# A hybrid encoder layer on one core: V kept in the scratch by pairs of heads, the third pattern's results by heads, and the gate from tanh

## The chip, the cores and the metric

The kernel runs on one core of one Trainium2 chip. The metric is the device time of one execution in microseconds (us). The times of before are the median of three runs; the profile is that of one more execution, taken by the hardware profiler, and has its own time.

## The reference: what is computed

One encoder layer over a sequence of 2048 tokens of width 1024, float32 in and out. The first third matters here: eight heads of width 64 attend in three dilated patterns, whose results are merged by their log-denominators, and beside them a gated depthwise convolution runs over 512 channels.

```python
DILATED_PATTERNS = ((128, 1), (512, 4), (2048, 16))

def dilated_sliding_attention(q, k, v):
    for window, d in DILATED_PATTERNS:
        half = window // (2 * d)
        o, lse = banded_attention(to_strided(q, d), to_strided(k, d), to_strided(v, d), half)
        outs.append(from_strided(o, d, B))
        lses.append(from_strided(lse, d, B))
    w = jax.nn.softmax(jnp.stack(lses, axis=0), axis=0)
    return jnp.sum(w[..., None] * jnp.stack(outs, axis=0), axis=0)

def conformer_conv(a, g, conv_w, conv_b, ln_g, ln_b):
    u = a * jax.nn.sigmoid(g)
    u = depthwise_conv(u, conv_w, width=31) + conv_b
    return jax.nn.silu(layernorm(u, ln_g, ln_b))
```

The rest is `h = x + [att || conv] W_out`, cross attention to 256 memory rows, a squared-ReLU MLP of width 4096 and a last RMSNorm.

## The kernel before

Nearly every product is made of three TensorE matmuls of 128x512 in a split of float32 into a high and a low part (`mm3`, L197 to L200): high by high, high by low, low by high. The work runs in stages, and within a stage generators are interleaved step by step (`weave`, L92); most of their steps are pinned behind the last TensorE instruction (`pinned`, L83), so that TensorE's order is the order of the code, while the other engines' queues are ordered when the program is built (`schedule_with_timeline_sim`, L1430).

- **Preparation** (about 0 to 218 us of the profile): the memory rows' products (`memory`), then x is transposed and split (`xprep`, L320), and the first gate halves (`glu`, L491) and the first q and k projections begin. `xprep` writes x back to the scratch in tiles `xts` from two buffers (L333 to L335). At its end `edges` (L710) zeroes the 256 rows before and after V in the scratch tensor `vtok` with two stores from one tile `zrow` of 16 partitions; `zrow` takes one of the two `raw` weight buffers, which the projections' weight loads use next.
- **Projections** (218 to 540): q, k and V (`lin_qk`, `lin_v` L544). V goes to the scratch as float16, for each head 65 columns of the high part (with a one for the denominator) and 65 of the low part: `VW` = 130 columns a head, 1040 a token, two bytes each. `lin_v` makes four heads (`g`) by 128 tokens (`t`) at a time and stores a block with rows of 1040 bytes (L576).
- **The first query block with the third pattern** (540 to 800): `att(0, far)` works through eight heads in pairs `pr`. For each head it does the third pattern over all 2048 tokens (`att_far`, L836) and the first and second pattern for the first 512 queries (`att_units`, L947). A unit is a chain over engines: scores on TensorE (L855, L856 or L992), mask and minimum on VectorE (L772), exp on ScalarE (L773), four transposes on TensorE (L779), high part on ScalarE (L782) and low part on VectorE (L783), products with V on TensorE (L787 to L789), and a copy out (L867, L869, L1010, L1012). The second halves of the gate (`glu` with tokens 1024 to 2047) and the first output weights are woven between (`rest`, L1100), and the first convolution block's layer norm with its Silu (L266).
- **Four blocks of 512 tokens** (`post`, L1204; 800 to the end): output projection, cross attention, MLP and last norm on TensorE, with the next block's attention (`att(p + 1)`) and convolution woven between.

What the change touches:

- `load_v` (L956) brings V for one pair of heads: the third pattern's as one transfer (L960), the first pattern's as five of 128 rows (L963 to L965), the second pattern's as eight (L968 to L971), one for each half `c` and residue `b`. Each run that is contiguous in the scratch is one token's two heads, 520 bytes.
- The third pattern's results go to `oscr[pr][1]` (L871), a tensor of 2048 tokens by both heads' 66 columns, one head and eight residues at a time, on ScalarE's own queue of transfers (ACTq); a contiguous run is 264 bytes. `combine` (L883) loads the second pattern's and third pattern's results as two transfers (L888 to L890).
- `glu` makes the gate with a Sigmoid on ScalarE (L508) and multiplies it on VectorE (L511); the convolution's weights `cw` (L160) come in `conv_unit` (L211).

Everything else goes through SyncE's queue (SPq, L57), in one order: weights, keys, queries, V, results. An instruction that issues a transfer holds its engine's queue until it may go.

Of the kernel before, what the change touches and what calls it, by code (L numbers as in the profile page):

```python
# [21 lines left out]
P = 128  # L22
S = 2048
D = 1024
H = 8
# [12 lines left out]
ROW = 66  # L38
VW = 130
VR = 8 * VW  # L40
# [7 lines left out]
def hybrid_layer(ctx, tc, A, out):  # L48
    nc = tc.nc
    ACT, DVE, POOL, PE = nc.scalar, nc.vector, nc.gpsimd, nc.tensor  # L50
# [5 lines left out]
    def dma(o, i, q=None):  # L56
        (q or nc.sync).dma_start(o, i)  # L57

    dr = pool("dram", DRAM)
# [16 lines left out]
    last = {}  # L76
# [30 lines left out]
    kscr = dr.tile([2, HD, H, 16, 160], F32R, name="kscr")  # L107
    qscr = dr.tile([2, HD, H, S], F32R, name="qscr")
    qfar = dr.tile([2, HD, H, 16, P], F32R, name="qfar")
    vtok = dr.tile([256 + S + 256, VR], F16, name="vtok")  # L110
    uscr = [dr.tile([P, 2080], F32, name=f"uscr{c}") for c in range(4)]
    xscr = [dr.tile([P, S], F32, name=f"xscr{k}") for k in range(KC)]
    cscr = [dr.tile([P, S], F32, name=f"cscr{c}") for c in range(4)]
    oscr = [[dr.tile([S, 2 * ROW], F32, name=f"oscr{p}_{q}") for q in (1, 2)] for p in range(4)]
    cath = [dr.tile([P, S], F32R, name=f"cath{k}") for k in range(KC)]
    catl = [dr.tile([P, S], F32R, name=f"catl{k}") for k in range(KC)]
    ascr = dr.tile([XH // 2, P, KC, 2 * NMEM], F32, name="ascr")
# [16 lines left out]
    cw = cst.tile([P, 4, 32], F32, name="cw")  # L134
# [10 lines left out]
    def setup():  # L145
        vecs, cwn = t2("vecs", F32, (64, P)), t2("cwn", F32, (32, DCONV))
        DVE.memset(vecs, 0.0)
        DVE.memset(cwn, 0.0)
        for nm, key in (("norm_mix_g", "mix"), ("norm_x_g", "x"), ("norm_mlp_g", "mlp"),
                        ("conv_b", "conv_b"), ("conv_ln_g", "ln_g"), ("conv_ln_b", "ln_b")):  # L150
            v = A[nm][0].rearrange("(k p) -> k p", p=P)
            dma(vecs[GV[key]:GV[key] + v.shape[0], :], v)
        dma(vecs[GV["final"]:GV["final"] + 8, :], A["norm_final_g"].rearrange("(k p) -> k p", p=P))
        dma(cwn[0:CW, :], A["conv_w"][0])
        pv = ps("c", "pvec")
        PE.transpose(pv[:, 0:64], vecs, ident[0:64, 0:64])
        for c in range(4):
            PE.transpose(pv[:, 64 + 32 * c:96 + 32 * c], cwn[:, c * P:(c + 1) * P], ident[0:32, 0:32])
        ACT.copy(gv, pv[:, 0:64])
        ACT.copy(cw.rearrange("p a b -> p (a b)"), pv[:, 64:192])  # L160

    def gain(key, k):
        if key == "mem":
# [114 lines left out]
    wp = pool("weights")  # L278
# [211 lines left out]

    def glu(c, ns, fine=False):  # L491

        sig = {}

        def unit(x, c0):
            raw = wp.tile([P, 8, P], F32, tag="raw", name=f"raw_{x}{c}{ns[0]}", bufs=2)
            dma(raw, wcols(w_in, c0))
            yield
            wh, wl = wsplit2(wp, raw, f"{x}{c}{ns[0]}", lo_eng=POOL)
            yield  # L500
            for n in ns:
                pt = ps("mm", "lin")
                for _ in linear_steps(pt, wh, wl, n):
                    if fine:
                        yield
                if x == "g":
                    sig[n] = t2(f"sig{c}_{n}")
                    ACT.activation(sig[n], pt, AF.Sigmoid)  # L508
                else:
                    u = t2(f"u{c}_{n}")  # L510
                    last["dve"] = DVE.tensor_tensor(u, pt, sig[n], op=ALU.mult)  # L511
                    dma(uscr[c][:, 15 + 512 * n:15 + 512 * (n + 1)], u)
                yield

        return unit("g", 3 * DATT + DCONV + c * P), unit("a", 3 * DATT + c * P)
# [28 lines left out]
    def lin_v(g, ns):  # L544

        raws = []
        for e in range(2):
            raws.append(wp.tile([P, 8, P], F32, tag="raw", name=f"raw_v{g}{e}", bufs=2))
            dma(raws[e], wcols(w_in, 2 * DATT + 256 * g + P * e))
        yield  # L550
        wh = lbv.tile([P, 8, 256], F32R, tag="wvh", name=f"wvh{g}{ns[0]}")
        wl = lbv.tile([P, 8, 256], F32R, tag="wvl", name=f"wvl{g}{ns[0]}")
        for e, raw in enumerate(raws):
            with ExitStack() as st:
                after(st, "pe")
                pc = ps("c", f"vbc{g}{e}")
                bcast_rows(pc, vmul[:, 2 * g + e:2 * g + e + 1], 1)
            DVE.tensor_tensor(raw, raw, pc[:, 0:P].unsqueeze(1).to_broadcast([P, KC, P]), op=ALU.mult)
            es = slice(e * P, (e + 1) * P)
            ACT.copy(wh[:, :, es], raw)  # L560
            POOL.tensor_tensor(wl[:, :, es], raw, f(wh[:, :, es]), op=ALU.subtract)
        yield
        for t in range(4 * ns[0], 4 * ns[-1] + 4):
            n, j = divmod(t, 4)
            pt = ps("mm", f"v{g}_{t}")[:, 0:256]
            for k in range(KC):
                sl = slice(j * P, (j + 1) * P)
                mm3(pt, XH_[k, n][:, sl], XL_[k, n][:, sl], wh[:, k, :], wl[:, k, :], k == 0, k == KC - 1)
            st = lbv.tile([P, 4, VW], F16, tag="vst", name=f"vst{g}_{t}", bufs=6)
            POOL.memset(st[:, :, HD:HD + 2], 1.0)  # L570
            p3 = pt.rearrange("p (h d) -> p h d", d=HD)
            ACT.copy(st[:, :, 0:HD], p3)
            last["dve"] = DVE.tensor_tensor(st[:, :, HD + 2:VW], p3, st[:, :, 0:HD], op=ALU.subtract)
            s2 = st.rearrange("p h e -> p (h e)")
            gs = slice(g * 4 * VW, (g + 1) * 4 * VW)
            dma(vtok[256 + P * t:256 + P * (t + 1), gs], s2)  # L576
            if t % 2:
                yield

# [128 lines left out]
        drain(*gens)  # L708

    def edges():  # L710
        zrow = wp.tile([16, 1, VR], F16, tag="raw", name="zrow", bufs=2)
        DVE.memset(zrow, 0.0)
        zb = zrow.to_broadcast([16, 16, VR])
        for t0 in (0, 256 + S):
            dma(vtok[t0:t0 + 256].rearrange("(q x) e -> q x e", q=16), zb)
        for c in range(4):
            dma(uscr[c][:, 0:15], zero[:, 0:15])
            dma(uscr[c][:, 15 + S:2080], zero[:, 0:17])
# [43 lines left out]
    aq = pool("att_q", side="right")  # L762
# [73 lines left out]
    def att_far(p2_, h, k, vt, q):  # L836

        pr, hh = divmod(h, 2)
# [3 lines left out]
        def unit(rq, qh, ql):  # L842
            if rq % 2 == 0:
                o8[0] = p2_.tile([P, 8, ROW], F32, tag="o3", name=f"o3_{h}{rq}", bufs=2)
            o2 = o8[0]
# [22 lines left out]
            else:  # L868
                DVE.tensor_copy(os_[:, :, 0:HD + 1], opt)  # L869
            if rq % 2:  # L870
                dma(oscr[pr][1].rearrange("(p r) (h e) -> p r h e", r=16, h=2)[:, 4 * rq - 4:4 * rq + 4, hh], o2,  # L871
                    nc.scalar)

        for rq in range(4):
            if rq == 0:
# [7 lines left out]
    def combine(p, pr, o0):  # L883
# [1 line left out]
        if p:  # L885
            yield
        ld = aq.tile([P, 2, 4, 2, ROW], F32, tag="ld", name=f"ld{p}{pr}")
        for i in range(2):  # L888
            dma(ld[:, i].rearrange("p j h e -> p j (h e)"),
                oscr[pr][i][512 * p:512 * (p + 1)].rearrange("(j p) e -> p j e", p=P))  # L890
        yield
        yield
        if p == 0:
# [33 lines left out]
        for i in range(3):  # L927
            src = ld[:, i - 1, :, :, 0:HD] if i else o0[:, :, :, 0:HD]
# [18 lines left out]
    def att_units(p, far, then):  # L947
# [4 lines left out]
        vt = {}  # L952
# [1 line left out]
        order = (1, 0) if far else (0, 1)  # L954

        def load_v(pr, pats):  # L956
            es = slice(pr * 2 * VW, (pr + 1) * 2 * VW)
            if 2 in pats and far:
                vt[2] = far.tile([P, 16, 2 * VW], F16, tag="v3", name=f"v3_{pr}")
                dma(vt[2], vtok[256:256 + S, es].rearrange("(i r) e -> i r e", r=16))  # L960
            if 0 in pats:
                vt[0] = aq.tile([P, 5, 2 * VW], F16, tag="v1", name=f"v1_{p}{pr}")
                for c in range(5):  # L963
                    t0 = 256 + 512 * p + P * c - 64
                    dma(vt[0][:, c], vtok[t0:t0 + P, es].rearrange("(i r) e -> r i e", r=16))  # L965
            if 1 in pats:
                vt[1] = aq.tile([P, 4, 2, 2 * VW], F16, tag="v2", name=f"v2_{p}{pr}")
                for c in range(2):  # L968
                    src = vtok[512 * (p + c):512 * (p + c) + 512, es].rearrange("(i a b) e -> b a i e", a=4, b=4)
                    for b in range(4):  # L970
                        dma(vt[1][:, b, c], src[b])  # L971

        def unit(pr, hh, pat, g, k, q_, opt, o0):
            if pat and not g and not hh:
# [5 lines left out]
            for z in range(2):  # L980
                blk = 2 * g + z
# [20 lines left out]
            for z in range(2):  # L1002
                blk = 2 * g + z
                for c in range(2):
                    vv = vt[1][:, blk, c] if pat else vt[0][:, blk + c]
                    att_pv(opt[0][:, blk], ph[:, 2 * z + c], pl[:, 2 * z + c], vv[:, hh * VW:(hh + 1) * VW],
                           c == 0, c == 1)
            if g:
# [2 lines left out]
                else:  # L1011
                    DVE.tensor_copy(os_[:, :, hh, 0:HD + 1], opt[0])  # L1012
            if g and hh and pat:
                dma(oscr[pr][0][512 * p:512 * (p + 1)].rearrange("(p b) e -> p b e", b=4),
                    os_.rearrange("p b h e -> p b (h e)"), nc.scalar)
            if g and hh:
                if pat == order[1]:
# [417 lines left out]
```

## Time and profile before

| | us |
|---|---|
| runs before, median of 3 (lowest to highest) | 2910.21 (2905.72 to 2911.84) |
| the profiled execution's own time | 2913.75 |
| its span, first to last instruction | 2912.0 |
| TensorE (PE) busy | 2840.1 |
| VectorE (DVE) busy | 1860.9 |
| ScalarE (ACT) busy | 1185.7 |
| GpSimd (POOL) busy | 456.9 |

How to read it: an instruction is named by engine, line of the kernel (a helper's line where a helper records it), operation, output tile and input tiles. "PE" is a matmul and "PEld" its weight load, which overlaps. "PEclk" is the share of TensorE's full clock that was granted in a stretch. The share of DMA is the mean busy share of the core's 16 DMA engines; a packet is one contiguous run. `SPq` and `ACTq` are the instructions with which SyncE and ScalarE issue transfers. `ACT_TABLE_LOAD` is an instruction that ScalarE runs ahead of a function whose table isn't loaded; the line beside it is that of the function. "A <- B" is an engine that sat idle until B had finished. The names of tiles have their numbers left out: `v<-vtok` are all loads of V, `oscr<-o` the stores of the second and third pattern's results.

### The profile page before, as it was taken

To read this page: it belongs to the slowest core of one execution; us is meant where nothing else is said; L and a number is where in the kernel's file an instruction comes from. 1 tells how busy PE (TensorE), PEld (TensorE's weight loads), DVE (VectorE), ACT (ScalarE), POOL (GpSimd) and SP (SyncE) were. 2 spreads that over 40 slices of the span, in tenths; PEclk is the share of its full clock that TensorE was granted. 3 is DMA by queue.
4 is the path that set the end of the run, shared out by engine and by line. 5 is a ranking of instruction groups with operands and counts; after the bars stand their busy time and mean duration, and the time that the engine had idled before them with its cause. 6 is when DMAs were issued, how large, how long until landed. Compare 5 with 4: busy or idle time off the path is not lost.

```text
span 2912.0 us, 41370 instructions
## 1 busy us (share of the span) xinstructions
PE 2840.1 (98%) x15628; PEld 2383.9 (82%) x15628; DVE 1860.9 (64%) x3311; ACT 1185.7 (41%) x2002; POOL 456.9 (16%) x502
## 2 busy tenths in 40 slices
PE   8989999989899999999999999999999999999999
PEld 7878899877688888888878888888888888888888
DVE  5636536455679886566887856589886555544445
ACT  5623211566444433433543334344333433432233
POOL 1336421121101111200021122001111200000000
PEclk9999999999899999999999999999999999999999
DMA  8979854798834544545344545534543445233332
GB/s 264 301 153 226 199 138 135 176 231 214 203 113 131 138 126 125 171 143 173 111 135 126 148 115 171 177 116 126 137 126 112 141 130 180 88 94 94 99 96 73
DMA packets 622271, 433.73 MB, mean 149 GB/s; under 512 B 191269, under 2 KB 553817, under 8 KB 622072
## 3 DMA queue, kind: packets, MB, share of 16 engines
q1 hardware_dynamic: 566904, 408.81, 50.1%
q10 hardware_dynamic: 55168, 22.29, 3.3%
q8 instruction: 123, 2.02, 0.3%
q14 instruction: 76, 0.62, 0.1%
HBM read 339.89 MB, written 91.11 MB: 148 GB/s over the span
## 4 chain that ended last, share of the span: by engine, by line
PE 82%; DVE 7%; DMA 4%; ACT 2%; issue 2%; SPq 1%; POOL 0%; ACTq 0%; POOLq 0%; DVEq 0%
PE dn L198 8%; PE dn L199 8%; PE dn L200 8%; PE up L198 7%; PE up L200 7%; PE up L199 7%; PE lin L198 3%; PE lin L199 3%; PE lin L200 3%; PE xs L198 2%; PE xs L200 2%; PE xs L199 2%; DVE cacc L215 2%; PE o L198 2%; PE o L199 2%
## 5 line engine op out<-in xcount | busy, mean ns | idle before, releaser
L199 PE MATMUL dn<-hhl,whi_d 128*128 128x512 f32 (+1 forms) x1056 | 402.9, 384 | 1.4 <-DVE hhl L1309 1.4
L198 PE MATMUL up<-mh,whi_u 128*128 128x512 f32 x1024 | 402.7, 393 | 0.8 <-DVE rl L1306 0.5
L198 PE MATMUL dn<-hhh,whi_d 128*128 128x512 f32 (+1 forms) x1056 | 401.6, 391 | 1.1 <-ACT hhh L1308 1.1
L200 PE MATMUL dn<-hhh,wlo_d 128*128 128x512 f32 (+1 forms) x1056 | 402.1, 384 | 0.0
L199 PE MATMUL up<-ml,whi_u 128*128 128x512 f32 x1024 | 399.7, 390 | 1.8 <-DVE ml L1199 1.8
L200 PE MATMUL up<-mh,wlo_u 128*128 128x512 f32 x1024 | 399.8, 391 | 0.0
L215 DVE SCALAR_TENSOR_TENSOR cacc<-cu,cw,cacc 128x512 f32<-128x512 f32 x480 | 388.8, 810 | 5.5
L189 ACT CAST whi_d<-raw_d 128x1024 fp32r<-128x1024 f32 x128 | 134.6, 1052 | 423.5 <-PE up L199 383.0
L1324 DVE TENSOR_TENSOR h<-h,dn 128x512 f32<-128x512 f32 (+1 forms) x264 | 172.3, 667 | 161.0 <-PE dn L200 159.7
L189 ACT CAST whi_u<-raw_u 128x1024 fp32r<-128x1024 f32 x128 | 134.4, 1050 | 327.6 <-PE dn L199 293.4
L1306 DVE SCALAR_TENSOR_TENSOR rl<-up,ssumx 128x512 f32<-128x512 f32 x128 | 88.0, 690 | 259.6 <-PE up L200 255.5
L198 PEld LDWEIGHTS dn<-hhh,whi_d 128*128 128x128 f32 x1056 | 197.7, 188 | 40.6 <-DVE h L1324 3.5
L200 PEld LDWEIGHTS dn<-hhh,wlo_d 128*128 128x128 f32 x1056 | 198.4, 188 | 39.3
L199 PEld LDWEIGHTS dn<-hhl,whi_d 128*128 128x128 f32 x1056 | 198.8, 188 | 37.8 <-DVE hhl L1309 2.3
L199 PEld LDWEIGHTS up<-ml,whi_u 128*128 128x128 f32 x1024 | 192.4, 188 | 41.1 <-DVE ml L1199 3.1
L200 PEld LDWEIGHTS up<-mh,wlo_u 128*128 128x128 f32 x1024 | 192.2, 188 | 40.1
L198 PEld LDWEIGHTS up<-mh,whi_u 128*128 128x128 f32 x1024 | 192.4, 188 | 39.2 <-DVE rl L1306 0.9
L773 ACT ACTIVATE sm<-sm,o 128x256 f32<-128x256 f32 (+1 forms) x384 | 160.3, 465 | 119.1 <-DVE o L772 107.4
L190 DVE TENSOR_TENSOR wlo_u<-raw_u,whi_u 128x1024 fp32r<-128x1024 f32 x128 | 162.6, 1270 | 28.7 <-ACT whi_u L189 28.4
L190 DVE TENSOR_TENSOR wlo_d<-raw_d,whi_d 128x1024 fp32r<-128x1024 f32 x128 | 160.1, 1251 | 23.7 <-ACT whi_d L189 23.5
L772 DVE CUSTOM_DVE_ANT_0 sm<-s,mask 128x256 f32<-128x256 f32 (+1 forms) x384 | 128.2, 374 | 67.3 <-PE s L992 37.5
L783 DVE TENSOR_TENSOR pl<-pt,ph 128x512 f16<-128x512 f32 x160 | 109.5, 686 | 61.6 <-ACT ph L782 60.9
(402 smaller groups left out, 6269.3 us busy)
## 6 DMA issues: line engine op xcount, KB each, us to landing
raw_u<-in_w_up_dram SPq DMA_DIRECT2D x128, 512.0 KB
raw_d<-in_w_down_dram SPq DMA_DIRECT2D x128, 512.0 KB
raw_o<-in_w_out_dram SPq DMA_DIRECT2D x32, 512.0 KB
raw_a<-ascr SPq DMA_DIRECT2D x32, 512.0 KB
raw_b<-bscr SPq DMA_DIRECT2D x32, 512.0 KB
v<-vtok SPq DMA_DIRECT2D x208, 65.0 KB
k<-kscr SPq DMA_DIRECT2D x24, 512.0 KB
k<-kscr SPq DMA_DIRECT2D x8, 1152.0 KB
```

Of the source, the lines that this page charges most:

```text
L189: ACT.copy(hi, raw)
L190: (lo_eng or DVE).tensor_tensor(lo, raw, f(hi), op=ALU.subtract)
L198: PE.matmul(o, lh, rh, start=first, stop=False)
L199: PE.matmul(o, lh, rl, start=False, stop=False)
L200: last["pe"] = PE.matmul(o, ll, rh, start=False, stop=end)
L215: DVE.scalar_tensor_tensor(acc, u[:, t:t + 512], cw[:, c, t:t + 1], acc, op0=ALU.mult, op1=ALU.add)
L772: last["dve"] = DVE.tensor_tensor_reduce(dst, so, mask[:, 256 * m:256 * m + nk], 1.0, 3e38, ALU.add, ALU.min, mn)
L773: last["act"] = ACT.activation(dst, dst, AF.Exp, bias=mn, scale=-1.0)
L783: DVE.tensor_tensor(pl, pt, ph, op=ALU.subtract)
L1306: last["dve"] = DVE.scalar_tensor_tensor(r, pt, 0.0, rsb, op0=ALU.max, op1=ALU.mult)
L1324: last["dve"] = DVE.tensor_tensor(hs[m][:, sl], hs[m][:, sl], pt, op=ALU.add)
```

## The change

V's scratch is laid out by pairs of heads, `[4, 2560, 260]`, in place of `[2560, 1040]`. The third pattern's load then has 16 tokens in one run of 8320 bytes for each partition, and the second pattern's is two transfers with runs of 2080 bytes in place of eight with runs of 520; the first pattern's five stay as they were. A store of `lin_v` has two runs of 520 bytes for each token in place of one of 1040. The zero rows are stored from 64 partitions in place of 16. The third pattern's results go to a tensor of their own by heads, so that a store has runs of 2112 bytes in place of 264, and `combine` loads them with one transfer for each head, with runs of 264 bytes. The gate is made as `(tanh(g / 2) + 1) * a`, which is twice the gated value, and the convolution's weights are halved.

```diff
-    vtok = dr.tile([256 + S + 256, VR], F16, name="vtok")
+    vtok = dr.tile([H // 2, 256 + S + 256, 2 * VW], F16, name="vtok")
...
-    oscr = [[dr.tile([S, 2 * ROW], F32, name=f"oscr{p}_{q}") for q in (1, 2)] for p in range(4)]
+    oscr = [dr.tile([S, 2 * ROW], F32, name=f"oscr{p}_1") for p in range(4)]
+    ofar = [dr.tile([2, S, ROW], F32, name=f"oscr{p}_2") for p in range(4)]
...
-        ACT.copy(cw.rearrange("p a b -> p (a b)"), pv[:, 64:192])
+        ACT.activation(cw.rearrange("p a b -> p (a b)"), pv[:, 64:192], AF.Copy, scale=0.5)
...
-                    ACT.activation(sig[n], pt, AF.Sigmoid)
+                    ACT.activation(sig[n], pt, AF.Tanh, scale=0.5)
...
-                    last["dve"] = DVE.tensor_tensor(u, pt, sig[n], op=ALU.mult)
+                    last["dve"] = DVE.scalar_tensor_tensor(u, sig[n], 1.0, pt, op0=ALU.add, op1=ALU.mult)
...
-            dma(vtok[256 + P * t:256 + P * (t + 1), gs], s2)
+            dma(vtok[2 * g:2 * g + 2, 256 + P * t:256 + P * (t + 1)].rearrange("r t e -> t r e"),
+                st.rearrange("p (r h) e -> p r (h e)", r=2))
...
-        zrow = wp.tile([16, 1, VR], F16, tag="raw", name="zrow", bufs=2)
+        zrow = wp.tile([64, 1, VR], F16, tag="raw", name="zrow", bufs=2)
         DVE.memset(zrow, 0.0)
-        zb = zrow.to_broadcast([16, 16, VR])
+        zb = zrow.to_broadcast([64, 4, VR])
         for t0 in (0, 256 + S):
-            dma(vtok[t0:t0 + 256].rearrange("(q x) e -> q x e", q=16), zb)
+            dma(vtok[:, t0:t0 + 256].rearrange("r (q x) e -> q r (x e)", q=64), zb)
...
-                dma(oscr[pr][1].rearrange("(p r) (h e) -> p r h e", r=16, h=2)[:, 4 * rq - 4:4 * rq + 4, hh], o2,
-                    nc.scalar)
+                dma(ofar[pr][hh].rearrange("(p r) e -> p r e", r=16)[:, 4 * rq - 4:4 * rq + 4], o2, nc.scalar)
...
-        for i in range(2):
-            dma(ld[:, i].rearrange("p j h e -> p j (h e)"),
-                oscr[pr][i][512 * p:512 * (p + 1)].rearrange("(j p) e -> p j e", p=P))
+        ts = slice(512 * p, 512 * (p + 1))
+        dma(ld[:, 0].rearrange("p j h e -> p j (h e)"), oscr[pr][ts].rearrange("(j p) e -> p j e", p=P))
+        for hh in range(2):
+            dma(ld[:, 1, :, hh], ofar[pr][hh, ts].rearrange("(j p) e -> p j e", p=P))
...
-                dma(vt[2], vtok[256:256 + S, es].rearrange("(i r) e -> i r e", r=16))
+                dma(vt[2].rearrange("i r e -> i (r e)"), vtok[pr][256:256 + S].rearrange("(i r) e -> i (r e)", r=16))
...
-                vt[1] = aq.tile([P, 4, 2, 2 * VW], F16, tag="v2", name=f"v2_{p}{pr}")
+                vt[1] = aq.tile([P, 2, 4, 2 * VW], F16, tag="v2", name=f"v2_{p}{pr}")
                 for c in range(2):
-                    src = vtok[512 * (p + c):512 * (p + c) + 512, es].rearrange("(i a b) e -> b a i e", a=4, b=4)
-                    for b in range(4):
-                        dma(vt[1][:, b, c], src[b])
+                    dma(vt[1][:, c].rearrange("p b e -> p (b e)"),
+                        vtok[pr][512 * (p + c):512 * (p + c) + 512].rearrange("(i a b) e -> a i (b e)", a=4, b=4))
...
-                    vv = vt[1][:, blk, c] if pat else vt[0][:, blk + c]
+                    vv = vt[1][:, c, blk] if pat else vt[0][:, blk + c]
```

More of the change, by code (lines that the diff above doesn't have):

```diff
@@ L573, in lin_v @@
             last["dve"] = DVE.tensor_tensor(st[:, :, HD + 2:VW], p3, st[:, :, 0:HD], op=ALU.subtract)
-            s2 = st.rearrange("p h e -> p (h e)")
-            gs = slice(g * 4 * VW, (g + 1) * 4 * VW)
-            dma(vtok[256 + P * t:256 + P * (t + 1), gs], s2)
+            dma(vtok[2 * g:2 * g + 2, 256 + P * t:256 + P * (t + 1)].rearrange("r t e -> t r e"),
+                st.rearrange("p (r h) e -> p r (h e)", r=2))
             if t % 2:
@@ L956, in load_v @@
         def load_v(pr, pats):
-            es = slice(pr * 2 * VW, (pr + 1) * 2 * VW)
             if 2 in pats and far:
                 vt[2] = far.tile([P, 16, 2 * VW], F16, tag="v3", name=f"v3_{pr}")
-                dma(vt[2], vtok[256:256 + S, es].rearrange("(i r) e -> i r e", r=16))
+                dma(vt[2].rearrange("i r e -> i (r e)"), vtok[pr][256:256 + S].rearrange("(i r) e -> i (r e)", r=16))
             if 0 in pats:
                 vt[0] = aq.tile([P, 5, 2 * VW], F16, tag="v1", name=f"v1_{p}{pr}")
+                t0 = 256 + 512 * p - 64
                 for c in range(5):
-                    t0 = 256 + 512 * p + P * c - 64
-                    dma(vt[0][:, c], vtok[t0:t0 + P, es].rearrange("(i r) e -> r i e", r=16))
+                    dma(vt[0][:, c], vtok[pr][t0 + P * c:t0 + P * c + P].rearrange("(i r) e -> r i e", r=16))
             if 1 in pats:
-                vt[1] = aq.tile([P, 4, 2, 2 * VW], F16, tag="v2", name=f"v2_{p}{pr}")
+                vt[1] = aq.tile([P, 2, 4, 2 * VW], F16, tag="v2", name=f"v2_{p}{pr}")
                 for c in range(2):
-                    src = vtok[512 * (p + c):512 * (p + c) + 512, es].rearrange("(i a b) e -> b a i e", a=4, b=4)
-                    for b in range(4):
-                        dma(vt[1][:, b, c], src[b])
+                    dma(vt[1][:, c].rearrange("p b e -> p (b e)"),
+                        vtok[pr][512 * (p + c):512 * (p + c) + 512].rearrange("(i a b) e -> a i (b e)", a=4, b=4))
         def unit(pr, hh, pat, g, k, q_, opt, o0):
@@ L1013, in unit @@
             if g and hh and pat:
-                dma(oscr[pr][0][512 * p:512 * (p + 1)].rearrange("(p b) e -> p b e", b=4),
+                dma(oscr[pr][512 * p:512 * (p + 1)].rearrange("(p b) e -> p b e", b=4),
                     os_.rearrange("p b h e -> p b (h e)"), nc.scalar)
```

## The prediction

> **What bounds the kernel now.** I read the page first, then busy times by stage, then, in the stages where TensorE idles, the chain of waits, the waits and the transfers. The page:
>
> ```profile
> span 2912.0 us, 41370 instructions
> ...
> PE 2840.1 (98%) x15628; PEld 2383.9 (82%) x15628; DVE 1860.9 (64%) x3311; ACT 1185.7 (41%) x2002; POOL 456.9 (16%) x502
> ```
>
> TensorE is busy in all but 72 us. The change adds and removes no matmul, so what it can move is those 72 us and the time in which TensorE runs at a lower clock. Busy times by stage (stretch, its length, busy time and count of PE, PEld, DVE, ACT, POOL, then PEclk, DMA share, GB/s) show where both lie:
>
> ```profile
> 145.00:218.00 73.00, 63.80 (x286) 52.00 (x285) 24.37 (x38) 20.47 (x31) 24.59 (x21) 0.91 0.73 154
> 218.00:515.00 297.00, 297.00 (x1682) 261.67 (x1681) 159.94 (x219) 71.07 (x126) 112.34 (x118) 1.00 0.69 173
> 515.00:540.00 25.00, 25.00 (x115) 20.86 (x114) 2.79 (x10) 4.86 (x7) 6.62 (x4) 1.00 0.99 217
> 540.00:745.00 205.00, 183.79 (x1606) 158.45 (x1604) 115.71 (x485) 137.14 (x307) 37.65 (x57) 0.96 0.86 211
> 745.00:800.00 55.00, 43.47 (x252) 34.54 (x251) 32.08 (x80) 23.03 (x43) 4.43 (x4) 0.84 0.86 192
> 800.00:2550.00 1750.00, 1743.19 (x9141) 1441.99 (x9140) 1259.34 (x2093) 726.16 (x1164) 228.40 (x261) 1.00 0.47 136
> ```
>
> From 218 to 540 PE has no gap, and from 800 to 2550 only 6.8 us of 1750. Two stages are open: 145 to 218 (9.2 us idle, clock 0.91) and 540 to 800 (21.2 and 11.5 us idle, clock 0.96 and 0.84). The lost clock of the second is about 205 x 0.04 + 55 x 0.16 = 17 us. What those stages gain stays gained: nothing after them waits for a fixed time, PE just starts its dense part earlier.
>
> **Part one: the zero rows of V.** The chain around 200 us (start, length, what):
>
> ```profile
> 180.97 12.44 DMA vtok<-zrow
> ...
> 203.66 4.52 DMA xscr<-xts
> ```
>
> and SyncE's waits, VectorE's waits, and three fine stretches:
>
> ```profile
> SPq L57 <- DMA vtok<-zrow: 7.5, 1, 7.5
> ```
> ```profile
> DVE xts L334 <- DMA xscr<-xts: 14.0, 2, 12.2
> ```
> ```profile
> 181.00:193.50 12.50, 12.50 (x65) 10.48 (x64) 7.17 (x10) 5.84 (x8) 6.15 (x5) 1.00 0.85 113
> ...
> 198.30:206.70 8.40, 0.37 (x3) 0.05 (x1) 1.35 (x2) 0.13 (x1) 0.00 (x0) 0.73 1.03 274
> 206.70:216.00 9.30, 8.13 (x23) 6.27 (x24) 4.55 (x7) 4.12 (x7) 6.82 (x6) 0.51 0.57 167
> ```
>
> The next weight load needs the buffer that `zrow` holds, so SyncE stands 7.5 us until the zeros have landed, and behind it in SyncE's queue stand the stores of `xts`, whose buffers VectorE needs back (12.2 us). PE sits out 8.0 us, then 1.2 us, and runs the 9.3 us after at half clock (0.51: 4.6 us more). While the zeros are moved, the 16 engines are 0.85 busy at only 113 GB/s. The price of their packets, and of packets of like size from a tile of 128 partitions (queue: packets, MB, share of 16 engines; first 181 to 193.5 us, then 895.5 to 899):
>
> ```profile
> q1 hardware_dynamic: 738, 1.40, 84.7%
> ```
> ```profile
> DMA  6979999996401026997999940000222323232222
> ...
> q10 hardware_dynamic: 134, 0.26, 19.6%
> ```
>
> The first is 12.5 x 0.847 x 16 / 738 = 229 ns a packet of some 1.9 KB, the second 3.5 x 0.196 x 16 / 134 = 82 ns for the same size. The new stores have the same number of packets and bytes (512 of 2080, 32 for each engine), from four times as many partitions. Bounds: nothing is gained if the slow price is that of a repeated source; from 12.44 us to 32 x 0.082 = 2.6 us, 9.8 us, if the landing is all packet time. I take the difference of the two prices, 32 x (229 - 82) = 4.7 us, between the ends. PE's gap shrinks by that, and I halve the 4.6 us at low clock with it: **7 us** (0 to 14). The memset has the same number of columns and costs the same. Next late is then `xprep`'s own stores, behind 3 of 8 us that are left.
>
> **Part two: Tanh for Sigmoid.** ScalarE's groups from 535 to 800 us:
>
> ```profile
> L773 ACT ACT_TABLE_LOAD x8 | 10.3, 1283 | 0.1
> L508 ACT ACT_TABLE_LOAD x6 | 7.7, 1283 | 0.1
> L266 ACT ACT_TABLE_LOAD x1 | 1.3, 1283 | 0.4 <-ACT o L867 0.4
> ```
>
> Every gate tile between the exps costs two loads, one ahead of it and one for the next exp. If Tanh lies in the table of exp, 13 of the 14 loads of the first two rows go (one exp still follows the Silu of L266): 13 x 1.283 = 16.7 us of ScalarE. If not, none goes. I take the first, since rows of this kernel show that a table holds several functions: copies and squares bring no loads between the exps. How much PE sees, by 10 us stretches, summed: first the eight with such loads (540, 560, 610, 620, 630, 640, 690, 710), then the other twelve from 550 to 740:
>
> ```profile
> sum 80.00, PE 67.58 PEld 56.00 DVE 41.64 ACT 61.28 POOL 11.77; mean PE 8.45 PEld 7.00 DVE 5.20 ACT 7.66 POOL 1.47
> ```
> ```profile
> sum 120.00, PE 111.20 PEld 97.86 DVE 70.49 ACT 73.28 POOL 25.89; mean PE 9.27 PEld 8.15 DVE 5.87 ACT 6.11 POOL 2.16
> ```
>
> PE idles 1.55 us in one of the eight, 0.73 in one of the twelve: 8 x 0.82 = 6.6 us, which is 31% of the stage's 21.2. The same share of its 8.2 us of lost clock is 2.6. Together **9 us**, 55% of the 16.7; bounds 0 and 16.7 + 2.6 = 19.
>
> By the Trainium skill ("ScalarE: Activation LUTs", "Table sets: the hidden batching unit") exp and tanh are in one set and sigmoid heads another, which no run here has shown; its section "What ACT_TABLE_LOAD costs" adds a drain of 1380 ns to each load, 2.66 us in all, and by that ScalarE would gain 35 us. The rows show no idle time beside the 1283 ns (0.1 us for eight), so the sum goes by 1.283.
>
> The gate's product costs the same: a two-operand product from PSUM against a three-operand operation from PSUM, 692 and 690 ns.
>
> ```profile
> L511 DVE TENSOR_TENSOR u<-lin,sig x16: 616/692/693, 155.0 to 744.9; 128x512 f32<-128x512 f32 x16
> ```
> ```profile
> L1306 DVE SCALAR_TENSOR_TENSOR rl<-up,ssumx 128x512 f32<-128x512 f32 x128 | 88.0, 690 | 259.6 <-PE up L200 255.5 <-ACT ssumx L1289 3.5
> ```
>
> The scaled copy of `cw` is one instruction in place of one.
>
> **Part three: the transfers.** SyncE's issues of V, the result loads, and ScalarE's waits for transfers from 535 to 800:
>
> ```profile
> L57 SPq DMA_DIRECT2D v<-vtok x212: 499/591/1737, 490.2 to 2199.2; - x106
> ```
> ```profile
> 657.82 7.41 SPq L57 DMA_DIRECT2D v<-vtok  x11
> 665.34 0.42 SPq L57 DMA_DIRECT2D uscr<-u  x1
> ```
> ```profile
> ACT sm L773 <- DVE o L772: 44.8, 39, 3.9
> ...
> ACT sm L773 <- DMA catl<-catl: 4.7, 1, 4.7
> ACT ph L782 <- DMA ql<-qfar: 4.2, 1, 4.2
> ACT sm L773 <- DMA uscr<-u: 4.0, 1, 4.0
> ...
> ACT ph L782 <- DMA v<-vtok: 3.2, 1, 3.2
> ```
> ```profile
> q10 hardware_dynamic: 17216, 5.41, 10.2%
> ```
>
> No `ph` or `sm` reads `ql`, `u`, V or `catl`. I read the four waits, 16.1 us, as ScalarE's own result stores (`oscr<-o`, in its instruction stream) held until an earlier transfer has landed; exps and casts stand behind them. Of 13 issues of V for a pair, 6 go at 0.59 us, and one load of results is added, which I price as an issue of V, 0.6 (above the 0.42 of `uscr<-u`): whatever stands behind in SyncE's queue goes 6 x 0.59 - 0.6 = 2.9 us earlier. The `uscr<-u` at 665.34, straight behind eleven issues of V, is one on which ScalarE is held. I give the 2.9 us to three of the four holds (`catl` isn't behind V): 8.8 us of ScalarE, 55% of it at PE: **5 us**. Bounds: all four go and PE sees all, 16; or more stores are held than now, the rival below.
>
> The packets themselves: ScalarE's queue moved 17216 in 265 us, 265 x 0.102 x 16 / 17216 = 25 ns each. The third pattern's 16 stores are 16384 packets of 264 B and become 2048 at 82 ns: 25.6 us of each engine become 10.5, and the share of 0.86 loses 0.06. I count it at nothing beside the holds. The second pattern's loads run on a quarter of the engines (share 0.2 to 0.3 at the end of the strip above, where they are alone); now 32 packets an engine, 2.6 us a load, 5.2 for both against 8 x 0.59 = 4.7 of issues: no gain, no loss, and after 800 us PE's dense work hides either. The third pattern's long runs, with no like in the rows, lie between their former time and a shorter one: nothing.
>
> What is added: `lin_v`'s 32 stores get twice the packets, 8 more an engine, at 25 ns 0.2 us a store, hidden by PE's 297 us of 297; without that cover 32 x 0.2 = 6 us. `combine`'s 512 packets become 1024 of 264 B, 1024 x 25 / 16 = 1.6 us, hidden but for the last pair before 790 us: 0 to 1.6 us, taken as nothing.
>
> The Trainium skill ("DMA: Bandwidth & Descriptors", "Specifications") speaks against this edit: under 512 B a transfer becomes a read-modify-write. The rows' 25 ns for 264 B against 82 for 2112 is 2.4 times the time for a byte; by the rule that last load costs 1.6 us more, and the sum would be 1.6 us less of a gain.
>
> **Sum.** 7 + 9 + 5 = 21 us: the profile's 2912.0 becomes 2891. That execution took 2913.75, 3.5 more than the median of the runs, so the runs come to 2910.21 - 21 = **2889 us**.
>
> **Rivals.**
>
> Absorbed: the exps wait 44.8 us in 39 waits for VectorE's minimum; if that chain fills the room, part one alone is left with 2 us of clock: -9, 2901. For it: these waits are the largest of ScalarE's, and the queues but TensorE's are ordered anew when the program is built. Against: PE idles twice as much where the loads stand.
>
> The change doesn't do what it says: Tanh brings as many loads as Sigmoid. Then 7 + 5 = 12, 2898.
>
> More: short gaps cost the clock, and with most gaps gone it stays at 1.00 from 540 to 800: 17 us, half of the 32.7 idle, and part one: 17 + 16 + 7 = 40, 2870. Against: the last 55 us wait for weights and queries that the change leaves alone.
>
> Slower: ScalarE's stores are held longer, behind transfers that now land late (a quarter of the engines, runs of 8320 B). A hold costs 16.1 / 4 = 4.0 us. Sixteen third-pattern stores stand there; with eight more held and PE seeing all, 32 - 16 (parts one and two) = +16, 2926. It decides from four more holds on. For it: four happen now. Against: fewer issues, less packet time.
>
> **How the numbers follow.** Chances: the forecast 0.50 (its own range 2880 to 2898), absorbed 0.17, no shared table 0.08, more 0.15, slower 0.10. The range of 2866 to 2908 takes in "more" and "absorbed" with some us at either end, and leaves out "slower" and a sum of all upper bounds (14 + 19 + 16 = 49, 2861). What a measurement can tell from no change is about 0.2%, 5.8 us: faster means under 2904.4. Forecast, no table, more and three quarters of absorbed: 0.86; the rest of absorbed is "same", 0.04, with some of it on both sides: 0.85, 0.06, 0.09.
>
> **What would show it.** Zeros: SyncE's wait for `vtok<-zrow` near 3 us, PE's idle time from 198 on under 5. Tanh: no load at L508 between exps, two or three in all from 535 to 800. Transfers: ScalarE's waits for transfers under 8 us there, ScalarE's queue near 2900 packets. PE's idle time from 540 to 800 should come from 32.7 to about 22. I am wrong if the loads stay, if ScalarE is held more often, or if PE's gaps come back elsewhere, after 800 above all.

## The result, and the profile after

The changed kernel took **2917.61 us** (median of 19 runs, 2910.3 to 2927.66) against 2910.29 (19 runs beside it, 2905.26 to 2914.15): a ratio of 1.0026 with the interval 1.0018 to 1.0035. It is 7.3 us slower, where 21 faster was predicted. The page of the profiled execution:

```profile
span 2919.0 us, 41303 instructions
...
PE 2837.9 (97%) x15628; PEld 2386.1 (82%) x15628; DVE 1859.8 (64%) x3311; ACT 1166.1 (40%) x1988; POOL 454.5 (16%) x502
```

TensorE has as much work as before and 81 us of idle time in place of 72. ScalarE does 20 us less and has 14 instructions fewer. The stages, with the columns of the table that the prediction opened with:

```profile
145.00:218.00 73.00, 69.14 (x320) 56.87 (x319) 25.78 (x39) 24.19 (x35) 29.48 (x26) 0.98 0.73 179
218.00:515.00 297.00, 295.01 (x1665) 259.74 (x1664) 158.13 (x217) 67.72 (x122) 108.40 (x116) 0.99 0.68 170
515.00:540.00 25.00, 25.00 (x121) 21.04 (x121) 4.06 (x19) 5.69 (x13) 6.62 (x4) 1.00 0.81 226
540.00:745.00 205.00, 179.43 (x1626) 157.66 (x1625) 118.48 (x481) 123.01 (x296) 37.54 (x57) 0.96 0.85 225
745.00:800.00 55.00, 42.34 (x241) 34.71 (x240) 31.96 (x75) 21.63 (x38) 4.38 (x4) 0.85 0.58 159
800.00:2550.00 1750.00, 1736.69 (x9084) 1435.82 (x9084) 1251.56 (x2084) 720.71 (x1158) 226.43 (x261) 1.00 0.45 135
```

The first stage came out as predicted: PE's idle time fell from 9.2 to 3.9 us and the clock rose from 0.91 to 0.98. From 218 to 515, where before had no gap, PE now idles 2.0 us. From 540 to 800 its idle time rose from 32.7 to 38.2, where 22 was expected, and from 800 to 2550 it doubled, from 6.8 to 13.3. Against the same instructions of before, the changed kernel is 2.5 us ahead when the third pattern begins, 6.2 ahead at 798 us and 6.7 behind at the end: almost 13 us go after 800.

What goes after 800 goes in three equal places, 4.2 us in each. One is shown: first what SyncE, ScalarE, VectorE and PE do (timeline: start, length, engine, what; in brackets the idle time before it), then the DMA engines from 1097.5 to 1105.5 us, 0.2 us to a digit:

```profile
1097.33 1.14 SPq L57 DMA_DIRECT2D v<-vtok  x2
1098.64 0.37 SPq L57 DMA_DIRECT2D raw_u<-in_w_up_dram  x1
...
1098.14 0.33 ACTq L57 DMA_DIRECT2D oscr<-o  x1
...
1105.33 0.43 DVE L773 CUSTOM_DVE_ANT_0 sm<-s,mask 128x256 f32<-128x256 f32 x1 [5.31 <-PE dn L201]
...
1105.80 0.91 ACT L774 ACTIVATE sm<-sm,o 128x256 f32<-128x256 f32 x2 [6.50 <-DVE o L773]
...
1109.77 0.79 PE L199 MATMUL dn<-hhh,whi_d 128*128 128x512 f32 x1 [2.41 <-DVE h L1323]
1110.36 0.63 PE L200 MATMUL dn<-hhl,whi_d 128*128 128x512 f32 x1
```
```profile
DMA  0000002229999322135799899999999922223222
...
q1 hardware_dynamic: 1012, 0.87, 44.8%
q10 hardware_dynamic: 144, 0.27, 10.2%
```

The same place before:

```profile
1102.10 5.81 SPq L57 DMA_DIRECT2D v<-vtok  x8
...
1102.91 0.33 ACTq L57 DMA_DIRECT2D oscr<-o  x1
...
1107.23 0.42 DVE L772 CUSTOM_DVE_ANT_0 sm<-s,mask 128x256 f32<-128x256 f32 x1 [2.44 <-DMA oscr<-o]
```

The second pattern's two loads are issued in 1.14 us instead of eight in 5.81. ScalarE's result store follows 0.8 us behind the first issue in both. VectorE's next mask needs the buffer which that store reads. (The profile puts this wait down to a matmul of `dn`, which the mask doesn't read; in all six places after 800 where the two loads are issued just ahead of the store, VectorE starts 0.6 to 0.7 us behind the store's last packet.) In the packet records the store's packets start between 1099.3 and 1104.5 us, 5.2 us for 264 KB, against 1104.1 to 1106.6 before; VectorE stands 5.3 us instead of 2.4. Of the store's 128 packets 96 have started by 1100.2, and the last 32 start from 1103.0 on; of its 16 closing packets of 4 bytes, twelve come by 1100.3 and four from 1104.5 on. So what comes late is a quarter of the store, the share of four engines. Before, that quarter started 1.0 us behind the rest, and here 2.8. The work that now comes late behind it on VectorE is `h<-h,dn`, which frees an accumulator, and PE loses 2.4 us and then runs matmuls of 0.63 us instead of 0.39 until its clock is back. The strip gives the reason: its digits of 2, ahead of the store's and weights' 9s and behind them, are the loads of V alone, four engines of 16 busy. They last past 1105 us.

Between 540 and 800 the queue behind the long loads shows at ScalarE's own stores, and in a wait of PE for V itself:

```profile
648.70 7.80 SPq L57 DMA_DIRECT2D v<-vtok  x5
...
661.28 0.35 ACTq L57 DMA_DIRECT2D oscr<-o  x1
661.68 0.91 ACT L774 ACTIVATE sm<-sm,o 128x256 f32<-128x256 f32 x2 [9.76 <-DMA v<-vtok]
```
```profile
ACT sm L774 <- DMA v<-vtok: 9.8, 1, 9.8
...
ACT ph L783 <- DMA v<-vtok: 6.9, 1, 6.9
```
```profile
PE opt L788 <- DMA v<-vtok: 7.2, 1, 7.2
```

ScalarE stands 9.8 us until a load of V has landed, and PE's gap of 7.0 us at 655 lies within it; the second such wait is 6.9 us. By the packet records it isn't a long load that lands there: the five loads of the first pattern, with runs of 520 bytes, were issued behind the two long ones. At the first place the long loads' packets run from 647.6 to 658.7 us and the short ones' until 661.1. The four holds before had 3.2 to 4.7 each, 16.1 us in all, and the two now have 16.7. PE's own wait for V, 7.2 us in the last stage, was 1.5 before.

### The profile page after: what moved, and what is told of

Read it like the earlier page. It is cut to its first block, busy times and chain, and to the rows that moved or that the text cites. A ratio compares the mean times of both kernels' runs of the same rounds, so it can differ in the third digit from the quotient of the medians.

```text
span 2919.0 us, 41303 instructions
## 1 busy us (share of the span) xinstructions
PE 2837.9 (97%) x15628; PEld 2386.1 (82%) x15628; DVE 1859.8 (64%) x3311; ACT 1166.1 (40%) x1988; POOL 454.5 (16%) x502
## 4 chain that ended last, share of the span: by engine, by line
PE 81%; DVE 8%; DMA 6%; issue 2%; ACT 2%; SPq 1%; POOL 0%; ACTq 0%; POOLq 0%; DVEq 0%
PE dn L199 8%; PE dn L200 8%; PE dn L201 8%; PE up L199 7%; PE up L200 7%; PE up L201 7%; PE lin L199 4%; PE lin L201 4%; PE lin L200 4%; DVE cacc L216 3%; PE xs L199 2%; PE xs L201 2%; PE o L199 2%; PE xs L200 2%; PE o L200 2%; PE o L201 2%
## 5 line engine op out<-in xcount | busy, mean ns | idle before, releaser
L177 POOL TENSOR_TENSOR nr<-st_v,mhalf 128x4 f32<-128x4 f32 (+1 forms) x13 | 13.4, 1029 | 853.5 <-DVE st_v L173 853.5
```

The costliest lines, as they stand in the source:

```text
L177: POOL.tensor_tensor(dst, v, mhalf.to_broadcast([P, v.shape[1]]), op=ALU.pow)
```

## The experiments

Theory 1: the second pattern's two loads lie on four engines in long runs; whatever is queued behind them there (ScalarE's stores, weights, results) lands late. Theory 2, the rival: two issues in place of eight let SyncE run ahead, and its next weight load travels beside the store. Each ratio is to the kernel before, run on the same chip. Differences in us between kernels are of their medians; where the two ran on different chips, taking their ratios instead shifts a difference by up to 4 us. Two transfers on all engines in another form, which the first expectation names, gave no result.

**The loads on all engines, and the old eight.** Both keep everything else of the change.

```diff
# v2_eight_on_all: by half and group of 32 partitions, runs of 2080 bytes, outermost count 32
+    src = vtok[pr][512 * (p + c):512 * (p + c) + 512].rearrange("(i a b) e -> a i (b e)", a=4, b=4)
+    for a in range(4):
+        dma(vt[1][32 * a:32 * a + 32, c].rearrange("p b e -> p (b e)"), src[a])
# v2_eight_on_four: by half and residue as before, runs of 520 bytes, outermost count 4
+    src = vtok[pr][512 * (p + c):512 * (p + c) + 512].rearrange("(i a b) e -> b a i e", a=4, b=4)
+    for b in range(4):
+        dma(vt[1][:, c, b], src[b])
```

> The changed kernel, with the second pattern's V in eight transfers, one for each half and each group of 32 partitions, runs of 2080 bytes, outermost count 32. Theory 1: as the run with two on all engines, 2890 to 2904. Theory 2: eight issues keep the weight load back as before the change, so the gaps after 800 us go too: 2895 to 2906. If this run gains and the one with two on all engines does not, theory 2 holds; if both gain alike, theory 1.

> The changed kernel with only the second pattern's loads as before the change: eight transfers with runs of 520 bytes, outermost count 4. Theory 1: the quarter of the engines is loaded again, but with packets of a quarter of the length and spaced by the issues; the store's wait goes back to the 2.4 us of before, the gaps after 800 us go: 2895 to 2905. Theory 2: the same. A third theory (the loss is in the results by heads, or in the order in which the queues come out for another reason): it stays at 2912 to 2920.

On all engines: **2878.86**, ratio 0.988 (0.9865 to 0.9895). The old eight: **2887.19**, 0.9913 (0.9899 to 0.9926). Both are faster than theory 1 had them. So the two long loads alone turn a gain into a loss: 30.4 us beside the old eight, 38.8 beside the same long runs on all engines. More than half of that is lost ahead of 800: matched by the same masks on VectorE, at 860 us of before the old eight is 25.9 us ahead of before and the changed kernel 6.2; at 2269 us the old eight is 26.9 ahead and the changed kernel 6.6 behind. The place of the stall, on all engines, and its DMA engines from 1072 to 1080 us:

```profile
1072.20 3.68 SPq L57 DMA_DIRECT2D v<-vtok  x8
...
1076.89 0.42 DVE L773 CUSTOM_DVE_ANT_0 sm<-s,mask 128x256 f32<-128x256 f32 x1 [1.99 <-PE s L992]
```
```profile
DMA  0000026259999994277444644587899999999995
```

No stretch of 2s is left, and VectorE waits for scores and no longer for the store. The stages of this kernel:

```profile
540.00:745.00 205.00, 192.31 (x1728) 167.37 (x1726) 127.75 (x503) 129.14 (x309) 39.85 (x59) 0.98 0.88 239
745.00:775.00 30.00, 22.87 (x103) 18.26 (x102) 22.23 (x47) 12.42 (x21) 2.14 (x2) 0.83 0.60 152
775.00:2520.00 1745.00, 1741.16 (x9139) 1442.40 (x9138) 1252.78 (x2089) 724.64 (x1161) 226.35 (x261) 1.00 0.46 136
```

PE idles 12.7 + 7.1 us in the first two rows, where the changed kernel has 25.6 + 12.7 in its own (540 to 745 and 745 to 800), and 3.8 in the last.

**Two loads on all engines, and two loads with pauses.** The first keeps two transfers and brings the outermost count to 128, by putting the keys of the second pattern in the order of the scratch (token ahead of residue; scores' columns and mask follow). The second keeps the two transfers of the change and adds six of 16 x 8 bytes behind them in the code, which nothing uses, so that SyncE would be as busy as with eight.

```diff
# v2_two_rows
+    dma(vt[1][:, c].rearrange("p b e -> p (b e)"),
+        vtok[pr][512 * (p + c):512 * (p + c) + 512].rearrange("(q b) e -> q (b e)", b=4))
# v2_two_spaced
+    for j in range(6):
+        dma(spc[:, j], vtok[pr][512 * p + 16 * j:512 * p + 16 * j + 16, 0:4])
```

> The changed kernel with the second pattern's keys taken with the token ahead of the residue, in the scores' columns, in the mask and in V's partitions alike: V's second pattern is then two transfers, each one contiguous block of 128 runs of 2080 bytes, outermost count 128. Theory 1 (what hurts is that two long transfers lie on a quarter of the engines): with two issues and all engines it gains as the run with eight issues on all engines (2878.9 us) did, 2873 to 2890, if the scores' matmuls cost the same with keys read in the other order. Theory 2 (what hurts is that SyncE is through 4.6 us sooner and lets a weight load beside the store): it stays at 2905 to 2920.

> The changed kernel with six transfers of 16 runs of 8 bytes, which nobody uses, issued behind the second pattern's two loads of V, so that SyncE issues eight again and the two long ones stay on a quarter of the engines. Theory 1: the long packets are as before, 2908 to 2922. Theory 2: the weight load comes as late as before the change, 2882 to 2898.

Two on all engines: **2886.64**, 0.9905 (0.989 to 0.992). Theory 2 falls with this run: the two loads are issued together, and the weight load follows them as in the changed kernel, yet the gain is there.

```profile
1077.66 0.82 SPq L57 DMA_DIRECT2D v<-vtok  x2
1078.97 0.38 SPq L57 DMA_DIRECT2D raw_u<-in_w_up_dram  x1
```

Theory 1 holds, though two on all engines is some 7 us behind eight on all. The key order may be part of that: its second-pattern score matmuls (`s<-k,qt`) take 321 ns against 300.

Two with pauses: **2940.72**, 1.0098 (1.0084 to 1.0112), outside what either theory gave. This run doesn't test theory 2, because the pauses don't come where they were meant to: when the program was built, all 96 of the small transfers were ordered ahead of 572 us. At the place of the stall the weight load follows V's two loads as in the changed kernel, and the time that the run lost beside the changed kernel, 22 of 23 us, is lost ahead of 860 us, where ScalarE stands once for a small transfer itself and PE idles 9.1 us behind that:

```profile
568.48 0.58 ACT L783 CAST ph<-pt 128x512 f16<-128x512 f32 x1 [13.49 <-DMA spc<-vtok]
...
1118.05 1.14 SPq L57 DMA_DIRECT2D v<-vtok  x2
1119.36 0.37 SPq L57 DMA_DIRECT2D raw_u<-in_w_up_dram  x1
```

**How much of it, by size.** Four transfers with runs of 1040 bytes, still on four engines.

```diff
# v2_four_on_four
+    src = vtok[pr][512 * (p + c):512 * (p + c) + 512].rearrange("(i a x b) e -> x a i (b e)", a=4, x=2, b=2)
+    for x in range(2):
+        dma(vt[1][:, c, 2 * x:2 * x + 2].rearrange("p b e -> p (b e)"), src[x])
```

> The changed kernel with the second pattern's V as four transfers, one for each half and pair of residues, runs of 1040 bytes, outermost count 4: between the changed kernel's two with runs of 2080 (2917.6 us) and the eight with runs of 520 (2887.2). Theory 1, with the harm in how many bytes are queued at once on the quarter of the engines: between the two, 2893 to 2910. If a long packet in itself does the harm and 1040 bytes are short enough, or if SyncE's issues of 2.4 us are enough to space them: 2885 to 2892. If any bundling does all the harm: 2911 to 2920.

**2907.3**, 0.9978 (0.9969 to 0.9987). On four engines: eight of 520-byte runs 2887.2, four of 1040 bytes 2907.3, two of 2080 bytes 2917.6. The bytes and the engines are the same in all three, so four engines alone don't make the loss; how much is put on them at once does. The packet records of the place shown agree. In all three kernels the store is issued behind two of V's loads, which are 130, 260 and 520 KB, and its last closing packet comes 1.6, 3.3 and 4.4 us behind the twelfth of 16. With eight loads on all engines it comes 0.1 us behind, and with two 0.3. Whether the bytes ahead or the length of a packet counts, these runs don't separate. Nor do they show whether the weight load, which travels beside the store with two and four loads but not with the old eight, adds to it; with two on all engines it follows V too, and the quarter isn't late.

**The parts alone.** The first is the change with the Sigmoid and whole weights back; the second and third are the kernel before with one part.

```diff
# gate_from_sigmoid
-    ACT.activation(sig[n], pt, AF.Tanh, scale=0.5)
+    ACT.activation(sig[n], pt, AF.Sigmoid)
# zeros_alone (on the kernel before)
-    zrow = wp.tile([16, 1, VR], F16, tag="raw", name="zrow", bufs=2)
+    zrow = wp.tile([64, 1, VR], F16, tag="raw", name="zrow", bufs=2)
# tanh_alone (on the kernel before)
-    ACT.activation(sig[n], pt, AF.Sigmoid)
+    ACT.activation(sig[n], pt, AF.Tanh, scale=0.5)
```

> The changed kernel with the gate from Sigmoid and the convolution's weights whole, as before the change. By theory 1 the stage from 540 to 800 us is held by transfers, so the table loads that come back are partly hidden: 0 to +9 us against the changed kernel, 2917 to 2927. If the tanh was worth its 9 us on its own: +9, 2927. If the new order of the queues that came with it did the harm: under 2912.

> The kernel before, with the zero rows stored from 64 partitions in place of 16 and nothing else. The prediction's term is 7 us (0 to 14); in the changed kernel the last transposes of x came 5.4 us earlier. With the share of that which lasts to the end: 2902 to 2907 beside 2910. If the gain of the other edits needs this one, or it is eaten in the stage from 540 to 800 us: 2907 to 2911.

> The kernel before with the tanh gate and the halved convolution weights alone. The prediction's term is 9 us (0 to 19); the edit was worth 11.6 in the changed kernel and 16.1 with eight loads on all engines. Alone, with the transfers of before: 2897 to 2905. If it gains only where V is spread over all engines: 2906 to 2912.

Sigmoid in the changed kernel: **2929.24**, 1.0052 (1.004 to 1.0065), a little above what was expected; the tanh is worth 11.6 us there (about 8 by the two ratios). Zeros alone: **2908.52** against 2913.17, 0.9985 (0.9976 to 0.9994): 4.7 us. Tanh alone: **2903.89** against 2913.59, 0.997 (0.9958 to 0.9982): 9.7 us. The chain of zeros alone, where before had 12.44 us of landing:

```profile
182.17 7.06 DMA vtok<-zrow
```

**The rest of the sum.** The first is zeros and V's edit alone (the change with the Sigmoid and the old results); the other two are eight on all engines with the old results or with the Sigmoid.

```diff
# zeros_and_v and all_old_results: third pattern's results as before
-    dma(ofar[pr][hh].rearrange("(p r) e -> p r e", r=16)[:, 4 * rq - 4:4 * rq + 4], o2, nc.scalar)
+    dma(ofar[pr].rearrange("(p r) (h e) -> p r h e", r=16, h=2)[:, 4 * rq - 4:4 * rq + 4, hh], o2, nc.scalar)
# zeros_and_v and all_sigmoid
-    ACT.activation(sig[n], pt, AF.Tanh, scale=0.5)
+    ACT.activation(sig[n], pt, AF.Sigmoid)
```

> The zero rows from 64 partitions and V by pairs of heads with its long runs for the second and third pattern, as in the changed kernel; Sigmoid and the third pattern's results stay as before the change. Against zeros_alone this is the cost of V's edit by itself. Theory 1, from the runs so far (two on four engines against eight on four: +30): +20 to +40, 2925 to 2945. If the harm came only together with the results by heads or the tanh: within 5 us of zeros_alone.

> Eight loads on all engines (2878.9 us), with the third pattern's results as before the change: one tensor for both heads, stores with runs of 264 bytes, one load with runs of 528. The prediction counted the packets at nothing beside the held stores: 2879 to 2884. If the stores' 25 us of engine time are felt in that stage: 2885 to 2895. If the loads with runs of 264 bytes cost more than the stores save: under 2877.

> Eight loads on all engines (2878.9 us), with the gate from Sigmoid as before the change. The prediction's term is 9 us, bounds 0 and 19; the same edit cost the changed kernel 11.6 us. Where transfers no longer hold the stage the table loads should show as much or more: 2888 to 2896.

Zeros and V: **2935.97**, 1.0073 (1.0061 to 1.0086): beside zeros alone on the same chip, V's edit costs 27.4 us. Old results: **2891.12**, 0.9924 (0.9911 to 0.9938), so results by heads are worth 12.3 us. Sigmoid: **2894.93**, 0.9937 (0.9924 to 0.9949), so the tanh is worth 16.1 with V on all engines.

**A faster version.** Eight on all engines, and zeros from 128 partitions in runs of 1040 bytes.

```diff
# all_zeros128
-    zb = zrow.to_broadcast([64, 4, VR])
+    zb = zrow[:, :, 0:VR // 2].to_broadcast([P, 4, VR // 2])
-            dma(vtok[:, t0:t0 + 256].rearrange("r (q x) e -> q r (x e)", q=64), zb)
+            dma(vtok[:, t0:t0 + 256].rearrange("r (q x) e -> q r (x e)", q=P), zb)
```

> Eight loads on all engines (2878.9 us), with the zero rows from 128 partitions, runs of 1040 bytes, the same bytes. A packet of 2080 bytes took 229 ns by the first price from 16 partitions and about half of it from 64; if the number of source partitions sets the pace, the landing is shorter again by some 2 us: 2875 to 2878. If 64 were enough, or half as long runs take it back: 2878 to 2881.

**2875.75**, 0.9867 (0.9854 to 0.9881): 37 us below the kernel before on that chip. Its interval overlaps with that of eight on all engines, so that the zeros from 128 partitions bring something more isn't shown. The landing of the zeros is no longer in its chain of waits between 145 and 225 us, where the wait for xprep's store now ends last:

```profile
195.85 4.28 DMA xscr<-xts
```

## Why the prediction was wrong

**The step that failed** is in part three: "now 32 packets an engine, 2.6 us a load, 5.2 for both against 8 x 0.59 = 4.7 of issues: no gain, no loss, and after 800 us PE's dense work hides either." Both halves were wrong. The price of 82 ns came from stores that have all 16 engines; on four engines the packets of the two loads run from 1098.7 to 1106.1 us in the place shown, 7.4 us or 116 ns for each of an engine's 64. And the step asked only when the loads themselves land; it did not ask who else has packets on those four engines, or stands behind them in SyncE's queue. ScalarE's store has packets there, and VectorE waits for it; the first pattern's loads stand behind them, and ScalarE's next store waits for these. After 800 us PE's work covers 2.4 us of that, not 5.3. The kernel before held a row that said so, of VectorE's waits over the whole span, and it was not used:

```profile
DVE sm L772 <- DMA oscr<-o: 12.5, 4, 5.1
```

So any growth of that store's landing was on the path already. The cost was 30.4 us, set against 0; of the 34 us between the two profiled executions about 20 came ahead of 800.

By the Trainium skill ("DMA: Bandwidth & Descriptors", in "Why a DMA increments its semaphore by 16 and not by 1") the number of engines is the largest up to 16 that divides the outermost counts of both sides: 4 here, 16 with counts of 32 or 128. The traces agree, with long stretches of 2s in one strip and none in the other, and with a quarter of the store late in one and not in the other.

**The rival that came** is the slower one, by its first mechanism: stores held behind transfers that land late on a quarter of the engines. Its size, 16 us on the far side of before, was twice what came, and its place was half wrong: it looked for more held stores of ScalarE from 540 to 800, where two were held in place of four, for as long in all, while 13 us of the loss came after 800, at VectorE. It also named the runs of 8320 bytes. No run takes that load back alone, but eight on all engines keeps it and is the better by 38.8 us, so the loss isn't due to it alone.

**The other terms, without the failed one**, are the kernel with the old eight loads: 24.3 us faster than before, where the sum's terms for it come to 7 + 9 = 16 (the 5 us of part three come from six issues fewer, which this kernel doesn't have). That the whole sum, 21, lies near 24.3 is luck. The terms:

- Zeros: 7 predicted, 4.7 measured. The price of 229 ns was a mean over all 738 packets of the queue; by the packet records the 512 of the zeros took 302 each. The landing went from 12.44 to 7.06 us, 5.4 against the step's 4.7; the halved clock loss was counted beside it, and by the time at the end that gain isn't there on top. SyncE's wait is 4.3 us, not 3:

```profile
SPq L57 <- DMA vtok<-zrow: 4.3, 1, 4.3
```

- Tanh: 9 predicted, 9.7 alone, 8 to 12 in the changed kernel, 16.1 with V on all engines. Two or three loads in the stage were foreseen, and two are left of 15:

```profile
L267 ACT ACT_TABLE_LOAD x1 | 1.3, 1283 | 0.4 <-ACT o L868 0.4
L774 ACT ACT_TABLE_LOAD x1 | 1.3, 1283 | 0.0
```

- Results by heads: packets counted at nothing, 12.3 measured with V on all engines. The prediction saw ScalarE's queue fall from 0.102 to near 0.06 of the engines, and it did:

```profile
q10 hardware_dynamic: 2880, 5.41, 5.9%
```

The freed time is that of 16 engines which are 0.86 busy in this stage, and the step set no price on it. That the shorter queues are what PE gained by is argued from this share, not shown apart. By the prediction's own prices the stores free 25.6 - 10.5 = 15.1 us of each engine, and the loads with shorter runs take 1.6 of it back.

- ScalarE's waits for transfers were to fall under 8 us, from 16.1, and are 16.7 for V alone (9.8 + 6.9). So the 5 us that part three put on them didn't come.

The range failed because the price of the loads had an end above (one the slower rival gave) and that end was left out of it with a chance of 0.10, though a row showed four engines and another showed VectorE waiting for the store.

**What stays open.** The parts measured one by one (4.7 + 9.7 + 12.3 = 26.7) are near the 24.3 of the old eight, but in other company their sizes differ by some 6 us, so what the third pattern's long runs and `lin_v`'s split rows cost or bring is within a few us and not known. Of the 20 us ahead of 800, PE's waits for `sm` (11.2 us from 540 to 800, 3.1 with the old eight) fit ScalarE's holds; how the rest divides isn't known. And no run holds the weight load back from the store with two long loads on four engines, so its part in the stall is open.

## What to carry to other kernels

Before fewer and longer transfers are counted as a gain, look at how many engines they lie on and which other queue's transfers share those engines; the price is paid by whoever waits for these, here VectorE and ScalarE. Cutting the load so that its outermost count was 32 in place of 4 was worth 39 us here, though it took eight issues in place of two. Where, as here, the engines' share is 0.86 and TensorE has gaps, saved packet time is a term of the sum; and a wait of a few us for a store in the earlier profile was one of the places where the slower transfer was felt. When a run adds instructions to delay something, look in its trace at where they came to stand.

## What the runs showed of the hardware

The same zeros, 512 packets of 2080 bytes, took by the packet records about 302 ns each from 16 partitions and 162 from 64; the landing fell from 12.44 to 7.06 us, and with 128 partitions it left the chain. So for these stores a packet's time depends on how many partitions the source is spread over, not on its size alone. And of the drain of 1380 ns that the Trainium skill ("ScalarE: Activation LUTs", "What ACT_TABLE_LOAD costs") puts beside each load of a table, nothing shows here: of the 15 loads from 535 to 800 us before, 14 have 17 or 18 ns of idle time ahead of them and 14 have 11 to 13 ns between the load and the function, and 13 loads fewer were worth at most 16.1 us, where their own time is 13 x 1.283 = 16.7. Last, the same 264 KB store had its last quarter 0.1 us behind the rest beside loads on all engines and 1.6, 3.3 and 4.4 us behind it beside 130, 260 and 520 KB issued ahead of it on four.
